# A macaron block on one Trainium2 core: feed-forward products by seven block products in place of eight

## The chip, the core and the metric

The kernel runs on one core of a Trainium2 chip. The time is device microseconds for one execution, the median of the runs shown. The engines are TensorE (PE), VectorE (DVE), ScalarE (ACT), GpSimd (POOL) and SyncE (SP, which issues DMAs). Each runs its own instructions in order; semaphores join them, and DMAs go through queues that SP, ACT or POOL feed.

## The reference

One sequence of 512 tokens with 1024 channels passes a feed-forward block, a mixer, a second feed-forward block and a last norm, all in float32:

```python
def swiglu(x, w_gate, w_up, w_down):
    return (jax.nn.silu(x @ w_gate) * (x @ w_up)) @ w_down
h = rms_norm(x, norm_ffn1[l])
x = x + 0.5 * swiglu(h, ffn1_gate[l], ffn1_up[l], ffn1_down[l])
...
x = x + mixed @ w_out[l]
h = rms_norm(x, norm_ffn2[l])
x = x + 0.5 * swiglu(h, ffn2_gate[l], ffn2_up[l], ffn2_down[l])
return rms_norm(x, norm_final)
```

The hidden width F is 2816, 22 tiles of 128. The mixer projects the normed rows with `w_in`, runs an RWKV-7 recurrence over 8 heads and a sliding-window attention side by side, and projects back with `w_out`; the change touches it only where its inputs come from.

## The kernel before

Each float32 factor of a product is split into a high part rounded to the matmul's format and a low part, the rest. A product is three matmuls into one PSUM bank (`mm3`, L452): high weights by high activations, high by low, low by high. Weights come in pieces of 512 KB (8 tiles of 128x128), loaded on SP's queue (`weights_load`, L402); ACT makes the high part (L409), DVE the low part (L410).

Channels lie on partitions, tokens along the free axis: a matmul holds a 128x128 weight tile and streams 128x512 activations. `ffn` (L467) goes over the hidden tiles in three parts (`PARTS`: 0 to 8, 8 to 16, 16 to 22). For each hidden tile it does the gate's and the up's eight k tiles, `gated` (L512) makes silu(gate) times up, split again; after a part, eight output tiles of down are accumulated and added to x (L508). The next norm's row sums ride along, and its scale is applied to gate and up. The last part of the second block is done in the layout of the output (`finish`, L530), with activations held and weights streamed, after transposing x (L541).

The order on PE, ACT and DVE is the program's (`MAN`); in the mixer PE's alone (`MAN1`). POOL's instructions are placed by the scheduler, so its 14 DMAs of small vectors (`vectors`, L153) go early though they stand late in the program. `want` and `take` keep two weight pieces ahead. In `start` (L207) the first tile's products (L252) are written in between the transposes of x (L233). `spill` (L595) and `unspill` keep x in memory across the mixer, as channels.

## Time and profile before

| | |
|---|---|
| runs | 1022.91, 1022.75, 1021.14 us; median 1022.75 |
| profiled execution | span 1023.7 us, which is its own time as far as the page tells it |
| first block | 0 to 376 us |
| mixer | 376 to 649 us |
| second block | 649 to 1023.7 us |

The page has the busy time of each engine over the span (part 1), its course in 40 slices with the granted PE clock in tenths, the share of the DMA engines and the rate (part 2), the queues (3), the chain of work that ended last (4), the costliest groups (5) and the DMA issues (6). A matmul's own time overlaps the next one's, so what one costs is the distance of two starts in the timeline. A wait is named by the instruction that waited and what released it.

### The profile page before, as it was taken

Reading aid. Unit: us, or ns where it says so; the run is one execution under the profiler, and the core shown is the slowest. Engines: PE = TensorE matmul, PEld = TensorE weight load, DVE = VectorE, ACT = ScalarE, POOL = GpSimd, SP = SyncE. Lnnn points to the kernel's source line nnn. Section 1 sums busy time; section 2 is a strip of 40 time slices with the busy share of each in tenths; the row PEclk is TensorE's granted clock in tenths of the full one; section 3 lists DMA queues with packets and bytes.
Section 4 is the critical chain, followed back from the end, with each engine's and each line's share of the span. In section 5 each row is a group of like instructions: output and inputs, shape, how many; then the busy total and the mean of one; then the engine's idle time right before and its main releaser. Section 6 shows DMA issues by size and latency. Waiting matters only on the chain. (4 is left out here: it accounts for less than half of the span.)

```text
span 1023.7 us, 12876 instructions
## 1 busy us (share of the span) xinstructions
PE 1008.6 (99%) x5123; PEld 824.8 (81%) x5123; DVE 557.8 (54%) x886; ACT 397.5 (39%) x631; POOL 52.2 (5%) x84
## 2 busy tenths in 40 slices
PE   8999999999999999999999999999999999999997
PEld 6888888888888887888867788788888888888886
DVE  5644424444344568799976686644443444424445
ACT  5422212332222447864376754432222322212343
POOL 6000000000000010120010120000000000000001
PEclk8999999999999999999989899999999999999999
DMA  8333333333233352313230323223333333333322
GB/s 207 103 101 87 100 103 92 94 103 101 85 102 93 103 176 62 94 51 78 77 84 22 93 63 103 81 87 101 102 97 88 103 101 88 101 103 90 96 83 83
DMA packets 174444, 96.82 MB, mean 95 GB/s; under 512 B 12334, under 2 KB 170096, under 8 KB 174384
## 3 DMA queue, kind: packets, MB, share of 16 engines
q1 hardware_dynamic: 172032, 90.19, 30.9%
q0 software_dynamic: 2336, 5.81, 2.0%
q8 instruction: 40, 0.66, 0.3%
q14 instruction: 20, 0.16, 0.1%
q10 hardware_dynamic: 16, 0.00, 0.0%
HBM read 89.43 MB, written 4.19 MB: 91 GB/s over the span
## 5 line engine op out<-in xcount | busy, mean ns | idle before, releaser
L457 PE MATMUL bpgu<-h_o,lo_bg 128*128 128x512 f32 x176 | 69.3, 394 | 0.0
L455 PE MATMUL bpgu<-h_o,hi_bg 128*128 128x512 f32 x176 | 69.2, 393 | 0.0
L456 PE MATMUL bpgu<-h_o,hi_bg 128*128 128x512 f32 x176 | 69.0, 392 | 0.0
L455 PE MATMUL apd<-h_a,hi_ad 128*128 128x512 f32 x176 | 68.6, 390 | 0.0
L456 PE MATMUL apd<-h_a,hi_ad 128*128 128x512 f32 x176 | 68.5, 389 | 0.0
L457 PE MATMUL apd<-h_a,lo_ad 128*128 128x512 f32 x176 | 68.5, 389 | 0.0
L457 PE MATMUL bpgu<-h_o,lo_bu 128*128 128x512 f32 x176 | 68.5, 389 | 0.0
L455 PE MATMUL bpgu<-h_o,hi_bu 128*128 128x512 f32 x176 | 68.5, 389 | 0.0
L456 PE MATMUL bpgu<-h_o,hi_bu 128*128 128x512 f32 x176 | 68.5, 389 | 0.0
L457 PE MATMUL apgu<-h_x,lo_au 128*128 128x512 f32 x168 | 65.5, 390 | 0.0
L455 PE MATMUL apgu<-h_x,hi_ag 128*128 128x512 f32 x168 | 65.5, 390 | 0.0
L455 PE MATMUL apgu<-h_x,hi_au 128*128 128x512 f32 x168 | 65.4, 390 | 0.0
L456 PE MATMUL apgu<-h_x,hi_au 128*128 128x512 f32 x168 | 65.4, 389 | 0.0
L457 PE MATMUL apgu<-h_x,lo_ag 128*128 128x512 f32 x168 | 65.4, 389 | 0.0
L456 PE MATMUL apgu<-h_x,hi_ag 128*128 128x512 f32 x168 | 65.4, 389 | 0.0
L409 ACT ACTIVATE hi_bu<-raw_bu 128x1024 fp32r<-128x1024 f32 x22 | 23.4, 1061 | 87.0 <-PE bpgu L456 78.3
L409 ACT ACTIVATE hi_au<-raw_au 128x1024 fp32r<-128x1024 f32 x21 | 22.3, 1062 | 83.0 <-PE apgu L456 70.1
L516 DVE TENSOR_TENSOR sgb<-bpgu,rstd 128x512 f32<-128x512 f32 x22 | 15.2, 692 | 70.6 <-PE bpgu L457 69.4
L516 DVE TENSOR_TENSOR sga<-apgu,rstd 128x512 f32<-128x512 f32 x22 | 15.2, 691 | 69.2 <-PE apgu L457 66.4
L409 ACT ACTIVATE hi_ad<-raw_ad 128x1024 fp32r<-128x1024 f32 (+1 forms) x24 | 23.8, 991 | 74.9 <-PE apd L456 51.9
L455 PE MATMUL bpd<-h_b,hi_bd 128*128 128x512 f32 x128 | 49.8, 389 | 0.0
L456 PE MATMUL bpd<-h_b,hi_bd 128*128 128x512 f32 x128 | 49.8, 389 | 0.0
(427 smaller groups left out, 2348.3 us busy)
## 6 DMA issues: line engine op xcount, KB each, us to landing
raw_bg<-in_ffn_gate_dram SPq DMA_DIRECT2D x22, 512.0 KB, 3.8
raw_bu<-in_ffn_up_dram SPq DMA_DIRECT2D x22, 512.0 KB, 3.8
raw_ag<-in_ffn_gate_dram SPq DMA_DIRECT2D x21, 512.0 KB, 3.9
raw_au<-in_ffn_up_dram SPq DMA_DIRECT2D x21, 512.0 KB, 3.8
raw_ad<-in_ffn_down_dram SPq DMA_DIRECT2D x16, 512.0 KB, 4.0
raw_bd<-in_ffn_down_dram SPq DMA_DIRECT2D x16, 512.0 KB, 4.0
raw_o<-in_w_out_dram SPq DMA_DIRECT2D x16, 256.0 KB, 3.3
raw_ad<-in_ffn_down_dram SPq DMA_DIRECT2D x8, 384.0 KB, 3.6
```

Of the source, the lines that this page charges most:

```text
L409: nc.scalar.activation(hi[:, :n], raw[:, :n], AF.Copy)
L455: nc.tensor.matmul(ps, hi[:, k], ah, start=first, stop=False)
L456: nc.tensor.matmul(ps, hi[:, k], al, start=False, stop=False)
L457: nc.tensor.matmul(ps, lo[:, k], ah, start=False, stop=last)
L516: nc.vector.tensor_tensor(sg, pg, self.rstd, ALU.mult)
```

## The change

Each feed-forward product is done as a product of 2x2 blocks by seven block products in place of eight, M1 to M7, in the order of `PRODUCTS`. The activations' blocks are two halves of the tokens by two halves of the contraction. For gate and up, the weights' block columns are up and gate, so one pass gives both; hidden columns go in chunks of 512 (the sixth has 256), and a chunk is 14 steps of 12 matmuls. Then down runs as a second phase over all chunks, product by product; its block columns are the two halves of the output. Activations are now held (128 tokens by 128 channels) and weights streamed, 512 columns at a time (`mm3w`).

The sums of weight blocks are not made by an engine: the block that stands in SBUF is the target of accumulating DMAs from memory on POOL's queue (`Stream.add`). W22 is added to W12 right after its load, for M7; W11 once M7's low part is made, for M6; W21 after M6's, for M4; and W12 to W11 after M1's, for M5. A step's piece is loaded nine steps ahead (`LOADS`; five or more in down), its high part made three ahead, its low part two. In down the loads, other than M3's, stand on POOL's queue too. Sums of activation blocks are made on POOL (`operand_sum`, `down_sums`).

Results come with tokens on partitions: hidden rows are transposed on PE (16 per chunk), the row sums of the norms come from ACT's squares along the free axis, x is kept and spilled by token and loaded again from memory in the down phase (`early`), and its rows are transposed for the mixer. POOL and SP now keep the program's order too. The small vectors are loaded in step 20 of the first block.

Three places in the instruction order, each with what it waits for. First POOL where the first block's down phase begins. `r12a83` is the tile for W12 of M7's first piece (step 83), `ds83` its operand sum, `r11a81` W11 of M1's fifth, `xN` the rows of x. Before, POOL's entries at the end of that block were these:

```order
L344 TENSOR_TENSOR ms_342<-ms_342,pack_123 128x4 [waits DVE_49,Activation_49,Pool_49]
L595 DMA x_spill_2609<-xT0_167 128x512 [waits DMASW3_49,DVE_49]
L595 DMA x_spill_2609<-xT1_183 128x512 [waits DMASW4_49,DVE_49]
L595 DMA x_spill_2609<-xT2_201 128x512 [waits DMASW5_49,DVE_49]
L595 DMA x_spill_2609<-xT3_217 128x512 [waits DMASW6_49,DVE_49]
```

and now:

```order
L698 TENSOR_TENSOR ds83_1847<-hTa0_474 128x512
L140 DMA r12a83_1872<-in_ffn1_down_dram 128x2x512
L131 DMA r12a83_1872<-in_ffn1_down_dram 128x2x512 [waits DMASW5_49,DMASW4_49]
L131 DMA r11a81_1811<-in_ffn1_down_dram 128x2x512 [waits DMASW0_49,DVE_49,Activation_49]
L698 TENSOR_TENSOR ds84_1878<-hTa1_755 128x512
L140 DMA r12a84_1895<-in_ffn1_down_dram 128x2x512 [waits DMASW7_49]
L131 DMA r12a84_1895<-in_ffn1_down_dram 128x2x512 [waits DMASW7_49]
L131 DMA r11a82_1842<-in_ffn1_down_dram 128x512 [waits DMASW1_49,DMASW2_49,DVE_49,Activation_49]
L605 DMA xN0_228<-in_x_dram 128x1024
L605 DMA xN1_229<-in_x_dram 128x1024 [waits DMASW3_49,PE_49]
```

A load (L140) is followed at once by its add (L131), which waits for a semaphore of POOL's DMA queue; the pattern comes six times, with two more rows of `xN` between.

Second PE at the small vectors (`vec_ps`, their transpose). `Ya1` is the bank of M2 in chunk 1, `Xa1` that of M6, which follows in step 20. Before:

```order
L457 MATMUL apgu_312<-h_x_240,lo_au_276 128x512
L157 MATMUL vec_ps<-pack,vec_rows 128x64 [waits DMASW4_49,DMASW5_49,DMASW3_49,DMASW6_49,DMASW2_49,DMASW7_49,DMASW1_49,DMASW0_49]
L455 MATMUL apgu_406<-h_x_139,hi_ag_308 128x512 [waits Activation_49]
```

and now:

```order
L637 MATMUL Ya1_1_602<-loa_163,AaM2h_233 128x512
L268 MATMUL vec_ps_634<-pack0_128,vec_rows_619 128x64 [waits DMASW4_49,DMASW3_49,DMASW5_49,DMASW2_49,DMASW6_49,DMASW1_49,DMASW7_49,DMASW0_49,DVE_49]
L635 MATMUL Xa1_0_507<-hia_161,AaM6h_273 128x512 [waits Activation_49]
```

and on POOL, where the 14 loads now stand between accumulates (`rawaa`) of chunk 1 and, behind them, of chunk 2:

```order
L131 DMA rawaa_112<-in_ffn1_up_dram 128x2x512 [waits DMASW6_49,DMASW4_49,DVE_49]
L131 DMA rawaa_112<-in_ffn1_up_dram 128x2x512 [waits DMASW7_49,DMASW5_49,DVE_49]
L264 DMA vec_rows_619<-in_norm_mix_dram 8x128 [waits PE_49]
L264 DMA vec_rows_619<-in_norm_ffn2_dram 8x128
L264 DMA vec_rows_619<-in_rwkv_shift_mix_dram 14x128 [waits DMASW2_49]
```

The transpose stands at much the same place on PE as before; its loads moved on POOL from ahead of the first block's work to behind the accumulates.

Third PE at the start, where `xta31` is the last of the eight groups of transposes of x and `Xa0_0` the first bank of M1. Before, the first three product matmuls stood ahead of the fourth group:

```order
L252 MATMUL apgu0_130<-h_x0_139,hi_ag0_104 128x512 [waits PE_49,Activation_49]
L252 MATMUL apgu0_130<-h_x0_139,hi_ag0_104 128x512 [waits DVE_49]
L252 MATMUL apgu0_130<-h_x1_149,hi_ag0_104 128x512 [waits Activation_49]
L233 MATMUL xt_ps3_169<-pack_123,xin2_109 128x128 [waits DMAHW7_49]
```

and now:

```order
L526 MATMUL xta21_202<-pack0_128,xin2_108 128x128 [waits DMAHW5_49]
L526 MATMUL xta21_202<-pack0_128,xin2_108 128x128 x3
L526 MATMUL xta31_208<-pack0_128,xin3_109 128x128 [waits DMAHW6_49,DVE_49]
L526 MATMUL xta31_208<-pack0_128,xin3_109 128x128 x3
L635 MATMUL Xa0_0_237<-hia_161,AaM1h_149 128x512 [waits DVE_49,Activation_49]
```

All transposes of x moved ahead of the first product. The diff, cut to its core:

```diff
-MAN = {PE, ACT, DVE}
-MAN1 = {PE}
-PARTS = [(0, 8), (8, 16), (16, 22)]
+MAN = {PE, ACT, DVE, POOL, SP}
+PRODUCTS = ("M1", "M7", "M2", "M6", "M5", "M3", "M4")
+LOADS, LOADS_D, HIGH, LOW, HI, LO = 9, 5, 3, 2, 5, 4
+SUMS_AHEAD = 5
+OPERANDS = {"M2": (0, 0), "M6": (1, 2), "M5": (4, 4), "M3": (5, 6), "M4": (8, 8)}
+MAN1 = {PE, POOL, SP}
...
+class Stream:
...
+        for c in range(6):
+            n = min(S, F - c * S)
+            nk = 1024 // n
+            for m in PRODUCTS:
+                for idx in range(4 // nk):
+                    add("gu", c, m, idx, nk, n, lambda i, j, c=c, n=n, nk=nk, idx=idx:
+                        rows((wu, wg)[j], i * S + idx * nk * P, nk, c * S, n))
+        self.first_down = len(self.pieces)
+        for m in PRODUCTS:
+            for c in range(6):
+                nk = 2 if c < 5 else 1
+                add("d", c, m, c, nk, S, lambda i, j, c=c, nk=nk: rows(wd, c * S + i * nk * P, nk, j * S, S))
...
+    def add(self, pc, b, i, j):
+        self.nc.gpsimd.dma_start(self.raw[pc.kind, pc.c, pc.idx, b], pc.block(i, j), accum_op=ALU.add)
+    def loads(self, upto, by=None):
+        while self.loaded < min(upto, len(self.pieces)):
+            pc = self.pieces[self.loaded]
+            self.loaded += 1
+            b = {"M1": "11", "M7": "12", "M2": "21", "M3": "22"}.get(pc.m)
+            if b:
+                eng = self.nc.gpsimd if pc.kind == "d" and pc.m != "M3" else by or self.nc.sync
+                eng.dma_start(self.tile(pc, b), pc.block(int(b[0]) - 1, int(b[1]) - 1))
+            if pc.m == "M7":
+                self.add(pc, "12", 1, 1)
+    def high(self, q):
+        while self.highs <= min(q, len(self.pieces) - 1):
+            self.loads(self.highs + 1)
+            pc = self.pieces[self.highs]
+            b = {"M1": "11", "M5": "11", "M2": "21", "M3": "22"}.get(pc.m, "12")
+            raw = self.raw[pc.kind, pc.c, pc.idx, b]
+            hi = self.ring("hi", HI, F32R).next(pc.n)[:, :pc.nk]
+            self.nc.scalar.activation(hi, raw, AF.Copy)
+            self.his[pc.q] = raw, hi
+            self.highs += 1
+    def low(self, q):
+        while self.lows <= min(q, len(self.pieces) - 1):
+            pc = self.pieces[self.lows]
+            raw, hi = self.his[pc.q]
+            lo = self.ring("lo", LO, F32R).next(pc.n)[:, :pc.nk]
+            self.nc.vector.tensor_tensor(lo, raw, hi.bitcast(F32), ALU.subtract)
+            self.parts[pc.q] = hi, lo
+            if pc.m in ("M7", "M6", "M1"):
+                self.add(pc, *{"M7": ("12", 0, 0), "M6": ("12", 1, 0), "M1": ("11", 0, 1)}[pc.m])
+            self.lows += 1
...
+        a = self.a = self.stream("a")
+        load(0, 0)
+        load(1, 0)
+        a.loads(2)
+        load(2, 0)
+        load(3, 0)
+        a.loads(4)
+        load(0, 1)
+        load(1, 1)
+        a.loads(6)
+        load(2, 1)
+        load(3, 1)
+        self.consts()
+        self.first_gain()
+        self.ss = self.small("ss_a", 4, "ss")
+        self.operands_begin("a")
+        gain = self.gain1
+        for h in range(2):
+            for t in range(4):
+                self.operand_turn(xin[t], t, h, gain)
+                if h == 0 and t < 2:
+                    self.operand_split("M1", t)
+                if h == 0 and t == 1:
+                    a.split(0)
+                    a.split(1)
+            if h == 0:
+                self.operand_sum("M7")
+                self.operand_split("M7")
+                a.split(2)
+        for t in range(4):
+            self.row_squares(xin[t], t)
+        self.row_scales()
...
+    def ffn(self, tag):
+        st = self.b if tag == "b" else self.a
+        self.due = []
+        self.banks = {}
+        self.hT = {}
+        self.temps = {}
+        self.gtr = Ring(self.f, "gt" + tag, 8, F32, S)
+        if tag == "a":
+            self.xN = self.new_rows()
+        n = len(st.pieces)
+        for q in range(n):
+            pc = st.pieces[q]
+            st.loads(min(q + LOADS, max(q + LOADS_D, st.first_down, 2 * q - st.first_down)))
+            st.high(q + HIGH)
+            st.low(q + LOW)
+            self.early(tag, st, q)
+            if pc.kind == "gu":
+                self.gu_step(st, pc)
+            else:
+                self.down_step(st, pc)
+            while self.due and self.due[0][0] <= q:
+                self.due.pop(0)[1]()
+    def early(self, tag, st, q):
+        for m, (a, b) in OPERANDS.items():
+            if q == a:
+                self.operand_sum(m)
+            if q == b:
+                self.operand_split(m)
+        if tag == "a" and q == 20:
+            self.vectors()
+        if tag == "a" and q == len(st.pieces) - 8:
+            self.consts_mix()
+        if q == st.first_down + 3:
+            if tag == "b":
+                self.xN = self.new_rows()
+            for t in range(4):
+                self.nc.gpsimd.dma_start(self.xN[t], self.I["x"][0, t * P:(t + 1) * P] if tag == "a" else self.xd2[t])
+        for k in range(st.first_down, len(st.pieces)):
+            if q == max(k - SUMS_AHEAD, st.first_down - 2):
+                self.down_sums(st.pieces[k])
+        k = q + LOW
+        if st.first_down <= k < len(st.pieces) or q == st.first_down - 1:
+            for k in range(st.first_down, k + 1) if q == st.first_down - 1 else (k,):
+                self.down_split(st.pieces[k])
+    def gu_step(self, st, pc):
+        nc = self.nc
+        m, c, tag = pc.m, pc.c, st.tag
+        hi, lo = self.A[m]
+        pieces = [p for p in st.group(pc)]
+        both = len(pieces) == 1
+        for i in (0, 1) if both else (pc.idx,):
+            b = self.bank(f"{tag}{c}", m, i)[:, :pc.n]
+            ts = slice(i * P, i * P + P)
+            first, last = m in ("M1", "M7", "M2"), m in ("M3", "M4", "M2")
+            k = 0
+            for p in pieces:
+                bh, bl = st.parts[p.q]
+                for kk in range(p.nk):
+                    self.mm3w(b, hi[:, k, ts], lo[:, k, ts], bh[:, kk], bl[:, kk], first and k == 0, last and k == 3)
...
+    def mm3w(self, ps, ah, al, bh, bl, first, last):
+        mm = self.nc.tensor.matmul
+        mm(ps, ah, bh, start=first, stop=False, skip_group_check=True)
+        mm(ps, al, bh, start=False, stop=False, skip_group_check=True)
+        mm(ps, ah, bl, start=False, stop=last, skip_group_check=True)
+    def down_sums(self, pc):
+        if pc.m not in ("M7", "M6", "M3"):
+            return
+        eng = self.nc.gpsimd
+        (a11, a12), (a21, a22) = self.down_blocks(pc.c)
+        if pc.m == "M7":
+            self.ds[pc.c] = self.f.tile([P, 2, 256], F32, tag="ds", name=f"ds{pc.q}", bufs=5)[:, :pc.nk]
+            eng.tensor_tensor(self.ds[pc.c], a11, a21, ALU.subtract)
+        elif pc.m == "M6":
+            eng.tensor_tensor(a21, a22, a21, ALU.subtract)
+            eng.tensor_tensor(a11, a11, a21, ALU.add)
+        elif pc.m == "M3":
+            eng.tensor_tensor(a12, a11, a12, ALU.subtract)
+    def down_step(self, st, pc):
+        m, c, tag = pc.m, pc.c, st.tag
+        first, last = m in ("M1", "M7", "M2"), m in ("M3", "M4", "M2")
+        if c == 0:
+            for i in range(2):
+                self.bank(f"{tag}d", m, i) if first else None
+        if c == 4:
+            return
+        todo = [(p, i) for i in range(2) for p in ((st.pieces[pc.q - 1], pc) if c == 5 else (pc,))]
+        for p, i in todo:
+            b = self.bank_of(m, i)
+            hi, lo = self.D[p.q]
+            bh, bl = st.parts[p.q]
+            ts = slice(i * P, i * P + P)
+            for kk in range(p.nk):
+                self.mm3w(b, hi[:, kk, ts], lo[:, kk, ts], bh[:, kk], bl[:, kk], first and p.c == 0 and kk == 0, last and p.c == 5)
+        if c == 5:
+            for i in range(2):
+                self.down_post(m, i)
+        if m == "M4":
+            (self.tail_a if tag == "a" else self.tail_b)(c)
...
+    def between(self, gain):
+        self.first_pts = []
+        ws = []
+        def part(i, ks):
+            for k in ks:
+                self.mm3(self.first_pts[i], ws[i], k, self.xh[k], k == 4, k == 3)
+        for i in range(2):
+            ws.append(self.take("in_" + RWKV_TILES[i][0]))
+            self.first_pts.append(self.psum("in_ps_" + RWKV_TILES[i][0]))
+            part(i, range(4, 8))
+        for j in range(4):
+            self.turn_rows(j, gain)
+        for t in (2, 3):
+            self.row_squares(self.xN[t], t)
+        self.row_scales()
+        part(0, range(4))
+        self.want()
+        self.stats_spread()
+        part(1, range(4))
```

## Rows read from the trace of the kernel before

**Rows 1.** The page's part 1, whole span: busy time, share and instructions of each engine.

```profile
PE 1008.6 (99%) x5123; PEld 824.8 (81%) x5123; DVE 557.8 (54%) x886; ACT 397.5 (39%) x631; POOL 52.2 (5%) x84
```

**Rows 2.** PE's waits, whole span: tile, line, releaser; total us, times, longest.

```profile
PE xt_ps L233 <- DMA xin<-in_x_dram: 3.4, 2, 2.3
...
PE pu L1036 <- ACT pack L1030: 0.2, 1, 0.2
```

**Rows 3.** PE's timeline late in block two: start, us, engine, line, operation, shapes, count.

```profile
954.89 0.39 PE L456 MATMUL bpgu<-h_o,hi_bu 128*128 128x512 f32 x1
...
957.16 0.39 PE L457 MATMUL bpgu<-h_o,lo_bu 128*128 128x512 f32 x1
...
980.51 3.65 PE L541 MATMUL xn_ps<-pack,xr 128*128 128x128 f32 x32
984.06 0.50 PE L548 MATMUL e<-hi_be,h_b 128*128 128x512 f32 x1
...
1012.79 0.28 PE L548 MATMUL e<-hi_be,h_b 128*128 128x256 f32 x1
...
1013.15 0.28 PE L548 MATMUL e<-hi_be,h_b 128*128 128x256 f32 x1
```

**Rows 4.** The page's part 2: DMA share in tenths and GB/s, 40 slices.

```profile
DMA  8333333333233352313230323223333333333322
GB/s 207 103 101 87 100 103 92 94 103 101 85 102 93 103 176 62 94 51 78 77 84 22 93 63 103 81 87 101 102 97 88 103 101 88 101 103 90 96 83 83
```

**Rows 5.** Busy by window: us, busy of each engine, PEclk, DMA share, GB/s.

```profile
6.00:12.00 6.00, 3.28 (x14) 2.62 (x15) 2.92 (x5) 2.67 (x5) 5.81 (x11) 0.70 1.19 280
12.00:20.00 8.00, 8.00 (x37) 6.56 (x37) 6.26 (x11) 5.73 (x11) 4.84 (x13) 0.80 1.16 267
26.00:90.00 64.00, 64.00 (x289) 52.78 (x288) 33.34 (x47) 22.78 (x30) 1.87 (x1) 1.00 0.34 99
566.00:570.00 4.00, 4.00 (x28) 2.71 (x27) 1.13 (x5) 3.35 (x12) 0.79 (x2) 0.77 0.92 326
```

**Rows 6.** Groups by line and form, ACT and DVE: busy us, mean ns, idle before.

```profile
L409 ACT ACTIVATE hi_bg<-raw_bg 128x1024 fp32r<-128x1024 f32 x22 | 23.3, 1061 | 51.2 <-PE bpgu L456 31.6 <-PE bpd L456 8.8 <-issue 7.1
...
L410 DVE TENSOR_TENSOR lo_bg<-raw_bg,hi_bg 128x1024 fp32r<-128x1024 f32 x22 | 27.0, 1225 | 41.3 <-ACT hi_bg L409 41.3
```

**Rows 7.** PE's timeline at the start: the first product, and the second tile's first.

```profile
10.14 1.63 PE L252 MATMUL apgu<-h_x,hi_ag 128*128 128x512 f32 x3
...
25.81 0.39 PE L455 MATMUL apgu<-h_x,hi_ag 128*128 128x512 f32 x1
```

**Rows 8.** POOL's timeline at the start, and one spill issue at the first block's end.

```profile
4.24 0.53 POOL L191 MEMSET pack<- 128x512 f32 x1
...
8.46 0.56 POOL L153 DMA_DIRECT2D vec_rows<-in_norm_mix_dram  x1
...
17.48 1.98 POOL L153 DMA_DIRECT2D vec_rows<-in_b_in_attn_dram  x4 [0.94 <-DMA lraw<-in_rwkv_a_dram]
...
352.81 0.54 POOL L595 DMA_DIRECT2D x_spill<-xT  x1 [2.55 <-DVE xT L508]
```

**Rows 9.** DMA issues: queue, count, KB each, median us from issue to landing.

```profile
raw_bg<-in_ffn_gate_dram SPq DMA_DIRECT2D x22, 512.0 KB, 3.8
...
xin<-in_x_dram SPq DMA_DIRECT2D x8, 256.0 KB, 5.8
x_spill<-xT POOLq DMA_DIRECT2D x8, 256.0 KB, 2.5
...
nf<-in_norm_final_dram POOLq DMA_DIRECT2D x1, 512.0 KB, 5.0
...
lraw<-in_rwkv_a_dram POOLq DMA_DIRECT2D x2, 128.0 KB, 6.2
g<-in_rwkv_g_dram POOLq DMA_DIRECT2D x1, 256.0 KB, 3.6
...
vec_rows<-in_b_in_attn_dram POOLq DMA_DIRECT2D x2, 0.5 KB, 3.8
```

More of the change, by code (lines that the diff above doesn't have):

```diff
@@ L155, in vectors @@
             r += k
[L156 removed]
+        pt = self.tp("vec_ps", (P, S))
         nc.tensor.transpose(pt[:, :n], raw, self.ident[:n, :n])
@@ L1273, in out_mix @@
+        x = self.xN[t][:, h * S:h * S + S]
+        self.nc.vector.tensor_tensor(x, self.wo[m], x, ALU.add)
     def out_mix(self, next_gain):
-        self.xh = []
-        for m in range(ND):
-            if m % 2 == 0:
-                w = self.take(f"o1_{m // 2}")
+        st = self.b = self.stream("b")
+        self.operands_begin("b")
+        self.ss = self.small("ss_b", 4, "ss")
+        self.xd2 = self.dram.tile([4, P, D], F32, name="x2_spill")
+        c = self.col[next_gain]
+        gain = self.vec[:, c:c + 8]
@@ new lines, in turn @@
+        def turn(m):
+            t, h = m % 4, m // 4
+            self.operand_turn(self.xN[t], t, h, gain)
+            if h == 0:
+                if t < 2:
+                    self.operand_split("M1", t)
+                if t == 3:
+                    self.operand_sum("M7", self.nc.vector)
+                    self.operand_split("M7")
+            else:
+                self.row_squares(self.xN[t], t)
+                self.nc.gpsimd.dma_start(self.xd2[t], self.xN[t])
+        w = {}
+        for m in range(8):
+            t, h = m % 4, m // 4
+            if t == 0:
+                for kp in range(2):
+                    w[kp] = self.take(f"o1_{2 * h + kp}")
+            ps = self.wo[m] = self.acc(f"wo1_{m}")
+            for k in range(4):
+                self.out_product(ps, self.mixed, w[k // 2], t, k, k == 0, k == 3)
+            if m in (0, 1) and self.plan:
@@ L1288, in block @@
         n.make_plan()
-        n.start(I["x"])
-        n.ffn("a", "norm_mix")
-        n.mixer("norm_ffn2")
-        n.ffn("b", None, I["ffn2_down"])
+        man = lambda: tc.manual_schedule(engines=MAN_F)
+        with tc.manual_schedule(engines=MAN1):
+            with man():
+                n.start(I["x"])
+                n.ffn("a")
+                n.between("norm_mix")
+            n.mixer()
+            with man():
+                n.out_mix("norm_ffn2")
+                n.ffn("b")
+                n.finish()
 _INS = ["x", "norm_ffn1", "ffn1_gate", "ffn1_up", "ffn1_down", "norm_mix", "w_in", "b_in_attn", "rwkv_shift_mix",
```

574 lines of the change are left out of this document (286 added, 288 removed).

## The prediction

> **What bounds the kernel now.** I read the page's busy times first. TensorE (PE) is busy for 99% of the span, its weight loads overlap it, and GpSimd (POOL) has 52 us of work in the whole run [rows 1]. The list of PE's waits comes second: the largest of its six entries is 3.4 us, on the loads of x at the start, the smallest 0.2, and all six make under 9 us [rows 2]. So time before is PE's products at their pitch, and whatever the change does to the time, it does either by the number of products or by making PE wait. The pitch comes from the timeline: eleven 128x512 matmuls start between 954.89 and 957.16, 0.227 us apart; 256-wide ones follow at 0.12, and 32 transposes of 128x128 fill the 3.55 us from 980.51 to 984.06, 0.111 each [rows 3]. Data is far from a limit: about 100 GB/s and a third of the DMA engines' time in the steady feed-forward stretch [rows 4], against 326 GB/s at a share of 0.92 in the busiest short stretch of the run [rows 5].
>
> I sum against the profiled execution (span 1023.7 us), which lies 0.95 us above the median of the three runs.
>
> **PE's work, -68 us.** Before, the feed-forward blocks issue 3150 matmuls of 512 columns and 36 of 256: 3150 x 0.227 + 36 x 0.12, with the unrounded 0.2267, is 718.4 us. After, each block has five chunks of 168, a last chunk of 168 at 256 columns, and 462 for down: 2604 and 336 in both, 630.6 us. That is -87.8. New transposes turn the products' results: 88 for each block's hidden rows and 32 for the rows that the mixer takes, 208; against them the 32 small matmuls of the old row sums and their spread leave. The net 176 x 0.111 is +19.5 [rows 3]. The later x transposes replace those of the old output part one for one. PE: **-68.3**.
>
> **Splitting the weights, nothing.** Each block now splits 119 pieces in place of 66, at 1.06 us on ScalarE (ACT) and 1.23 on VectorE (DVE) [rows 6]. In a chunk of 14 steps, 38.1 us of products and 1.8 of transposes, that is 15 and 17 us, and with evacuations of half that size neither passes 25 of 39.9. PE's products cover it, and HIGH and LOW put it three and two steps (8 and 5 us) ahead. If a weight arrives late, this cover is gone and 2.3 us lie on the path.
>
> **Start, +9.** Before, the first tile's 48 products (10.9 us) begin at 10.14, between arriving halves of x, and are done at 25.81: 14.9 us lost [rows 7]. After, all eight groups of transposes stand ahead of the first product on PE, and the last two loads of x are queued on SP behind six weight pieces. Until then 2.1 MB of x, 3.1 MB of weights and 1.05 MB of accumulates move; at 280 GB/s [rows 5] this is 22.4 us after an issue at about 1.6, so the first product comes at 24 in place of the 14.9: +9. Without the accumulates it is +5; with them read twice at 267 GB/s, +14.
>
> **Small vectors, +12.** Fourteen DMAs of vector rows were issued on POOL from 8.46 to 19.46 us, 0.51 each and 11.0 with POOL's own waits, and hidden: PE's transpose of them came later and waited for nothing [rows 2, 8]. Now they are issued in step 20 of the first block, in program order behind accumulates that wait for VectorE, and PE's transpose vec_ps stands between the products of step 19 and 20. So PE waits for all: 11.0 + 3.8 landing [rows 9] less one step of head start, 2.7: **+12.1**. Behind it the next accumulates are late, which the steps ahead still cover. Lower end: 7.1 of pure issue with two steps of start, 5.5.
>
> **Down phase, +29 for each block.** Here POOL is in order. For each of M7's six pieces it forms an operand sum, issues the load of W12, waits until that load has landed, and only then issues the add of W22 and whatever comes next. Between PE's arrival at down and M7's last piece stand 21 DMA issues at 0.55 (11.6, from the 0.54 of a spill issue [rows 8]), five and a half operand sums, six landings, the last add's landing, and its split (2.3). For the sums the trace has no row; a memset of the same tile takes 0.53 [rows 8], a sum reads two tiles, so I take 1.06 and 5.8 in all. With L for a landing this chain is 19.7 + 7L. PE has M1's products (15.0) and M7's first four pieces (10.9) to do meanwhile, 25.9, so it waits 7L - 6.2 in each block. Nothing on ACT, SP or DVE is late instead: M2's loads come next in POOL's queue and are due one chain later.
>
> L is bounded by rows of POOL's queue: 2.5 for a spill (256 KB, to memory), 3.6 for g (256 KB into SBUF), 5.0 for nf (512 KB into SBUF), 6.2 for lraw in the busy first microseconds [rows 9]. A weight piece is 512 KB into SBUF, as nf, so I take 5.0: 28.8 each, **+57.6**; the ends are 11.3 and 37.2 each. The Trainium skill, page "DMA: Bandwidth & Descriptors", section "Anatomy of one DMA - SWDGE (gpsimd) path", fits about 2.0 us plus bytes/436e3, 3.2 us for such a piece; by it the waits would be 16.2 each and the sum 25 us lower, 1031. The trace's nf, at 5.0, does not agree with that, so it stays outside my sum.
>
> **Traffic in gate/up, +10.** A chunk now moves 4.2 MB of loads and 4.2 MB of accumulates in 39.9 us, 211 GB/s in place of 99 [rows 5]. If an add costs what a load costs, this is 60% of the 354 GB/s that 326 at 0.92 stands for, and nothing waits but an occasional late piece: lower end 0. If an add costs two loads, the same chunk is worth 12.6 MB: 36 us at 354 GB/s, but 45 us at the 280 of the start [rows 5], which is 5.1 us for each of eleven full chunks, +56. I take **+10**, nearer to the first: adds have three steps (8.2 us) from their issue until ScalarE reads the sum, and the loads of the busy start land in 5.8 [rows 9].
>
> **Between blocks, +6; clock, +7.** After the last down product the mixer's rows are turned, scaled twice and squared: eight 128x512 copies at half of 1.06, two squares at 1.06, two evacuations at half of 1.23, 7.5 us, of which the first projections' 24 products (5.4) can hide some: 2 to 7.5, taken 6. After PE's idle time at the start the granted clock was 0.70 over 6 us and 0.80 over the next 8 [rows 5], means between the full 2.4 GHz and the 1.2 below it, and 1.8 and 1.6 us of full speed lost. Four long waits (vectors, two downs, the mixer) at 1.7 are +7; ends 2 and 20.
>
> **Sum:** -68.3 + 9 + 12 + 57.6 + 10 + 6 + 7 = +33, that is 1057 against the span of 1023.7, and **1056** against the median.
>
> **Rivals.** *The POOL chain is short (faster).* With all else as taken the change breaks even at 2 x (7L - 6.2) = 24, L = 2.6; with adds that cost nothing extra and no clock lost (-15) at L = 3.7. For it: g lands in 3.6 and the weights' own loads on SP in 3.8 [rows 9]. Against it: POOL's only 512 KB load took 5.0 in a quieter stretch than this. With L = 2.5 and neither extra it gives 1007. Chance 0.25. *Adds pace the gate/up stretch.* A sum in place must read what it adds to, so its bytes may count twice: +56 in place of +10, and adds that land in 7.5 cost down another 5: 1108. The Trainium skill, page "Collectives: The Full Stack", part 3, on why ReduceScatter is half of AllGather, says that an add takes two source reads on one ring and so runs at half the rate; that speaks against this change, and by it this rival holds. No row before shows an add at all. For it otherwise: the share is already 1.19 in the start at 280 GB/s [rows 5]. Against: a 36 us chunk would still fit under 39.9. Chance 0.17. *No change to be measured*: the waits just eat the 68 us saved, 0.03. That the change does not do what it says I exclude: the counts above are those of the built program. My forecast keeps 0.55.
>
> **Range.** About 0.2% is what a measurement can tell here. Faster takes the first rival, 0.25; same 0.03; slower the rest, 0.72. Low ends with L = 3.6 (start +5, vectors +5.5, down +38, nothing for traffic, +2, +2) give 1008; high ends (traffic +56, L = 6.2) 1120. From 1003 to 1130 leaves out some 0.1 on either side.
>
> **What would show it.** Right: PE busy near 940 us, waits listed on M7's products in both down phases near 29 us each, released by VectorE's lo and behind it by a POOL DMA; a gap of some 12 us at vec_ps; POOL's timeline with a load, an idle stretch of L, an add, six times over. Wrong: down phases with gaps under 12 us each (L overrated); gate/up steps that wait all along at a DMA share near 1 (the second rival); or PE's pitch itself changed.

## The result and the profile after

The changed kernel takes 1171.49 us (median of four runs, 1169.9 to 1176.27) against 1022.39 for the kernel before on the same chip: a ratio of 1.148 [1.145, 1.1511]. The direction was predicted, the size was not: 1056 had been forecast, at most 1130. The profiled execution has a span of 1174.6 us. Against the span before and the 68.3 us of products saved, 1174.6 - 1023.7 + 68.3 = 219 us of loss has to be found where the prediction had 102.

The page of the changed kernel, parts 1 and 2:

```profile
span 1174.6 us, 13568 instructions
PE 1004.7 (86%) x5053; PEld 805.1 (69%) x5053; DVE 711.2 (61%) x990; ACT 569.8 (49%) x891; POOL 325.0 (28%) x314
PE   5796999998357798699999999989999998446897
PEclk9797999999668898799998999989999999767989
DMA  9597798937777621512211153978988947868601
```

Three things differ from [rows 1]. PE is idle for 170 us where it was idle for 15. It is also busy for 1004.7 us where the count of products gave 940, so its instructions took 65 us longer; the clock's digits are low just where PE's are. And POOL has six times its old work. PE's list of waits, its longest entries (us in total, times, longest):

```profile
PE Qad L635 <- ACT dd L561: 32.4, 6, 8.3
PE Qbd L635 <- ACT dd L561: 29.7, 5, 9.4
PE Xbd L635 <- ACT dd L561: 12.4, 2, 11.4
PE gain_ps L237 <- POOL pack L224: 10.8, 1, 10.8
PE Xad L635 <- ACT dd L561: 10.6, 2, 9.7
PE vec_ps L268 <- DMA vec_rows<-in_b_in_attn_dram: 10.3, 1, 10.3
PE Xad L635 <- DVE xN L743: 6.9, 1, 6.9
PE Xbd L635 <- DVE xN L743: 6.7, 1, 6.7
...
PE Yb L637 <- DVE lob L160: 4.1, 1, 4.1
```

In [rows 2] the longest was 3.4. `Qad` and `Qbd` are M7's banks in the two down phases, which M4 uses again (2.2 of the 32.4 us lie there; M7 has five long waits in either block); `Xad` and `Xbd` are first M1's (released by ACT's split of an activation block, `dd`), later M6's (released by `xN`). By stretch (length, then PE, PEld, DVE, ACT and POOL busy, granted clock, DMA share, GB/s):

```profile
21.00:76.00 55.00, 45.78 (x184) 35.38 (x182) 36.81 (x39) 33.06 (x42) 22.04 (x15) 0.88 0.80 187
76.00:129.00 53.00, 42.68 (x184) 34.63 (x182) 23.46 (x25) 21.97 (x28) 16.31 (x23) 0.87 0.75 164
130.00:170.00 40.00, 40.00 (x186) 33.09 (x185) 23.39 (x25) 21.95 (x29) 9.62 (x9) 1.00 0.92 210
275.00:312.00 37.00, 20.49 (x80) 14.88 (x78) 11.62 (x16) 8.42 (x15) 16.95 (x18) 0.85 0.83 176
312.00:368.00 56.00, 29.26 (x67) 20.11 (x68) 17.51 (x16) 11.48 (x16) 29.40 (x28) 0.65 0.83 213
383.00:438.00 55.00, 47.36 (x200) 38.12 (x199) 46.89 (x46) 26.07 (x37) 24.86 (x33) 0.94 0.43 84
1025.00:1080.00 55.00, 28.89 (x68) 19.91 (x69) 17.44 (x16) 11.17 (x16) 30.21 (x28) 0.63 0.79 192
```

These are chunk 0, chunk 1, a steady chunk, M1 of down, M7 of down, M6 with M5 and M3, and M7 of the second block. A steady chunk takes 40.0 us with PE busy throughout, as the prediction's 39.9 has it. So the saving is there; the other rows are where more than three times as much is lost. From the first matmul of each stage in the timeline, against a product at full pitch (15.0 us for 66 matmuls):

| stretch | at full pitch | took | loss | the prediction's term |
|---|---|---|---|---|
| start and chunk 0 | 14.9 + 40.0 | 21.5 + 54.5 | 21.1 | +9 |
| chunk 1, with the small vectors | 40.0 | 53.4 | 13.4 | +12 |
| other gate/up, both blocks | | | 13.6 | +10 |
| M1 of down | 2 x 15.0 | 37.0 + 38.4 | 45.4 | 0 |
| M7 of down | 2 x 15.0 | 55.3 + 54.5 | 79.8 | +57.6 |
| M6, M5, M3 of down | 2 x 45 | 54.9 + 54.6 | 19.5 | 0 |
| M2, M4 of down | 2 x 30 + 1.4 | 39.1 + 31.2 | 8.9 | 0 |
| mixer | 273.1 | 292.9 | 19.8 | +6 |
| clock (in the rows above) | | | | +7 |

The sum is 221 against the 219 of the spans. Down alone is 154.

POOL's queue in M7 of the first block, from its timeline (start, duration, idle time before and what ended it):

```profile
313.43 0.75 POOL L140 DMA_DIRECT2D r12a<-in_ffn_down_dram  x1 [3.03 <-DVE dd L562]
318.75 2.51 POOL L131 DMA_DIRECT2D r12a<-in_ffn_down_dram  x2 [4.57 <-DMA r12a<-in_ffn_down_dram]
320.28 2.28 POOL L698 TENSOR_TENSOR ds<-hTa 128x512 f32<-128x512 f32 x1
321.49 1.76 POOL L140 DMA_DIRECT2D r12a<-in_ffn_down_dram  x1
329.24 2.43 POOL L131 DMA_DIRECT2D r12a<-in_ffn_down_dram  x2 [6.00 <-DMA r12a<-in_ffn_down_dram]
...
339.73 1.19 POOL L131 DMA_DIRECT2D r12a<-in_ffn_down_dram  x1 [6.08 <-DMA r12a<-in_ffn_down_dram]
```

It is the predicted pattern: operand sum (L698), load (L140), about 6 us of idle time until it lands, add (L131). A round takes 10.5 us, for 2.5 us of products. By the prediction's prices (3.5 issues of 0.55, a sum of 0.97 on the average, L of 5.0) it would be 7.9. The load at 313.43 came 3.0 us later still, behind VectorE. And on PE, what a wait does to the products behind it: the fourth of the six pieces from 347.23, half of the fifth behind it, the last from 361.30.

```profile
347.23 0.80 PE L635 MATMUL Qad<-hia,dd 128*128 128x512 f32 x1 [5.04 <-ACT dd L561]
...
349.41 0.63 PE L636 MATMUL Qad<-hia,dd 128*128 128x512 f32 x1
349.83 0.63 PE L637 MATMUL Qad<-loa,dd 128*128 128x512 f32 x1
...
353.42 0.39 PE L635 MATMUL Qad<-hia,dd 128*128 128x512 f32 x1
353.65 0.40 PE L636 MATMUL Qad<-hia,dd 128*128 128x512 f32 x1
...
361.30 0.79 PE L635 MATMUL Qad<-hia,dd 128*128 128x512 f32 x1 [7.02 <-ACT dd L561]
```

The pitch behind the wait is 0.43, nearly twice that of [rows 3], at a granted clock of 0.50 (348 to 351 us). It comes back to 0.23 from 351.89 on, with eight products left until the next wait; behind the three waits before this one it stays at 0.43 up to the last of the twelve products or the one before.

What these waits name is ACT's split of an activation block (`dd`), not a weight. ACT's order has the split for a piece behind the high part of the next piece's weights (`high` runs three steps ahead, the splits two), and that high part waits until its load or add has landed. ACT's rows in the first block, and one of PE's:

```profile
288.34 0.63 ACT L151 ACTIVATE hia<-r11a 128x512 fp32r<-128x512 f32 x1 [1.02 <-DMA r11a<-in_ffn_down_dram]
300.69 1.06 ACT L151 ACTIVATE hia<-r12a 128x1024 fp32r<-128x1024 f32 x1 [11.20 <-DMA r12a<-in_ffn_down_dram]
301.65 0.40 ACT L561 ACTIVATE dd<-hTa 128x256 fp32r<-128x256 f32 x1
302.11 0.79 PE L635 MATMUL Xad<-hia,dd 128*128 128x512 f32 x1 [9.68 <-ACT dd L561]
...
350.92 0.63 ACT L151 ACTIVATE hia<-r12a 128x512 fp32r<-128x512 f32 x1 [3.74 <-DMA r12a<-in_ffn_down_dram]
359.89 1.06 ACT L151 ACTIVATE hia<-r21a 128x1024 fp32r<-128x1024 f32 x1 [7.82 <-DMA r21a<-in_ffn_down_dram]
360.85 0.40 ACT L561 ACTIVATE dd<-ds 128x256 fp32r<-128x256 f32 x1
```

M1's last weights had their high part at 288.34, but its last products waited until 302.11, when M7's first add had landed. M7's last weights had theirs at 350.92, but the products waited until 361.30, when M2's first piece had landed. The second block has the same two waits, of 11.4 and 4.0 us.

### The profile page after: what moved, and what is told of

The parts are those of the page before. It is cut to its first block, busy times and chain, and to the rows that moved or that the text cites. A ratio compares the mean times of both kernels' runs of the same rounds, so it can differ in the third digit from the quotient of the medians.

```text
span 1174.6 us, 13568 instructions
## 1 busy us (share of the span) xinstructions
PE 1004.7 (86%) x5053; PEld 805.1 (69%) x5053; DVE 711.2 (61%) x990; ACT 569.8 (49%) x891; POOL 325.0 (28%) x314
## 5 line engine op out<-in xcount | busy, mean ns | idle before, releaser
L160 DVE TENSOR_TENSOR loa<-rawaa,hia 128x1024 fp32r<-128x1024 f32 x55 | 68.2, 1253 | 13.6 <-ACT hia L151 9.6
L160 DVE TENSOR_TENSOR lob<-rawab,hib 128x1024 fp32r<-128x1024 f32 x55 | 67.3, 1236 | 13.1 <-ACT hib L151 7.8
L151 ACT ACTIVATE hia<-rawaa 128x1024 fp32r<-128x1024 f32 x55 | 57.3, 1051 | 31.9 <-DMA rawaa<-in_ffn_up_dram 16.9
L151 ACT ACTIVATE hib<-rawab 128x1024 fp32r<-128x1024 f32 x55 | 57.4, 1051 | 30.8 <-DMA rawab<-in_ffn_up_dram 14.9
L562 DVE TENSOR_TENSOR dd<-ds,dd 128x512 fp32r<-128x512 f32 (+1 forms) x12 | 10.5, 874 | 93.2 <-ACT dd L561 93.2
L131 POOL DMA_DIRECT2D rawab<-in_ffn_gate_dram x22 | 27.2, 1248 | 115.8 <-DVE lob L160 47.8
L131 POOL DMA_DIRECT2D rawaa<-in_ffn_gate_dram x22 | 27.5, 1255 | 110.3 <-DVE loa L160 54.0
L635 PE MATMUL Xbd<-hib,dd 128*128 128x512 f32 x88 | 37.0, 421 | 19.2 <-ACT dd L561 12.4
L635 PE MATMUL Qad<-hia,dd 128*128 128x512 f32 x44 | 24.0, 546 | 32.4 <-ACT dd L561 32.4
L635 PE MATMUL Xad<-hia,dd 128*128 128x512 f32 x88 | 36.5, 415 | 17.4 <-ACT dd L561 10.6
L131 POOL DMA_DIRECT2D rawaa<-in_ffn_up_dram x22 | 26.8, 1230 | 74.7 <-DVE loa L160 54.6
L131 POOL DMA_DIRECT2D rawab<-in_ffn_up_dram x22 | 26.8, 1250 | 69.9 <-DVE lob L160 58.8
L562 DVE TENSOR_TENSOR dd<-hTb,dd 128x512 fp32r<-128x512 f32 (+1 forms) x31 | 29.1, 942 | 22.1 <-ACT dd L561 22.1
L562 DVE TENSOR_TENSOR dd<-hTa,dd 128x512 fp32r<-128x512 f32 (+1 forms) x31 | 29.8, 963 | 19.9 <-ACT dd L561 19.9
L160 DVE TENSOR_TENSOR lob<-rawbb,hib 128x1024 fp32r<-128x1024 f32 x22 | 26.9, 1222 | 19.3 <-ACT hib L151 19.3
L636 PE MATMUL Xad<-hia,dd 128*128 128x512 f32 x88 | 36.3, 412 | 1.9 <-DVE dd L562 1.1
L635 PEld LDWEIGHTS Qad<-hia,dd 128*128 128x128 f32 x44 | 11.4, 260 | 37.8 <-ACT dd L561 35.3
```

Source lines behind the costliest of these rows:

```text
L131: self.nc.gpsimd.dma_start(self.raw[pc.kind, pc.c, pc.idx, b], pc.block(i, j), accum_op=ALU.add)
L151: self.nc.scalar.activation(hi, raw, AF.Copy)
L160: self.nc.vector.tensor_tensor(lo, raw, hi.bitcast(F32), ALU.subtract)
L562: nc.vector.tensor_tensor(lo, src, hi.bitcast(F32), ALU.subtract)
L635: mm(ps, ah, bh, start=first, stop=False, skip_group_check=True)
L636: mm(ps, al, bh, start=False, stop=False, skip_group_check=True)
```

## The experiments

The first theory was that down is bound by POOL's order: loads, adds and sums in one queue, each add behind a landing. The rival was that the adds' bytes bind the DMA engines, in whatever order they are issued. Runs 1 to 8 are one execution each, so a difference of a few microseconds between them says little; the kernel before took 1021.23 beside 1, 2, 3 and 5, and 1019.18 beside 4, 6, 7 and 8.

**1. M7's and M2's loads from SP.** Nothing else moves; POOL still waits for each landing, but the next loads are under way meanwhile.

```diff
-eng = self.nc.gpsimd if pc.kind == "d" and pc.m != "M3" else by or self.nc.sync
+eng = {"M1": self.nc.gpsimd, "M7": self.nc.sync, "M2": self.nc.sync, "M3": self.nc.sync}[pc.m] if pc.kind == "d" else by or self.nc.sync
```

> In the down phases the loads of W12 (M7) and W21 (M2) go on SP's queue, M1's stay on POOL's; all accumulates stay where they are. Theory 1 (POOL's order: load, wait for its landing, add, six times over): the add finds its load landed, M7 falls from 55 us towards 25 in each block, the whole from 1171 to about 1110. Theory 2 (traffic: accumulates keep the DMA engines at a share of 0.8 in M1 and M7 whatever the order): M7 stays above 45 us, the whole above 1150, with the share of the DMA engines unchanged or higher.

Measured 1113.32: 58 us less. M7 fell from 55.3 and 54.5 to 25.8 and 28.1. M1 and M7 of the first block by window, and M7's waits, in this run:

```profile
274.00:308.00 34.00, 24.18 (x77) 16.94 (x77) 13.27 (x17) 9.06 (x16) 19.63 (x20) 0.75 1.09 290
308.00:334.00 26.00, 19.05 (x67) 13.99 (x67) 13.99 (x16) 10.66 (x15) 13.52 (x12) 0.87 1.03 201
PE Qad L635 <- ACT dd L561: 8.7, 3, 5.3
```

The waits on M7's bank fell from 32.4 to 8.7 us with the same bytes moved (2.2 of either in M4). So the order of the loads did cost most of M7's loss. M1 gained only 3.1 and 4.6 us, and the DMA share is now over 1: the next limit is already in sight.

**2. M1's loads off POOL as well**, from ACT's queue (`"M1": self.nc.scalar`).

> As the run before, and M1's loads in down are issued on ACT's queue, so that none of the down phase's loads stands in POOL's order. Theory 1: M1 falls too, from 37 us towards 20 in each block, the whole to about 1080. Theory 2: the bytes are the same, so M1 and M7 together stay above 80 us of the 92 in each block.

Measured 1120.04, no gain over the first run. M1 went from 33.9 to 31.1 and 33.8 to 30.5, not to 15; gate/up became longer (253.2 to 257.0, 230.4 to 235.9), perhaps by ACT's issues, which no run tried apart. M1 with all its loads free of POOL still takes twice its products, and the trace shows why. Its largest wait, 7.9 us in the first block, is the one of ACT's order: M1's last high part was made at 290.25, then ACT waited 9.2 us for M7's first piece, and the split of M1's last block came behind it.

**3. The adds of down cut to 16 of 512 columns**, order kept: nearly the whole sum of weight blocks is left out in down, and so are its bytes.

```diff
+        if pc.kind == "d":
+            raw, src = raw[:, :, 0:16], src[:, :, 0:16]
```

> The accumulates of the down phases add 16 of 512 columns only: the sums of the weight blocks are left out except there, the order, the number of DMAs and all waits stay. Theory 1: POOL still waits for each load, only the landing is shorter (from 6.5 towards 4 us without an add ahead of it in the queue), so M7 falls from 55 to about 40 us and the whole to about 1135. Theory 2: without the bytes M7 and M1 come near their 15 us of products, 20 to 25 each, the whole to about 1060.

Measured 1130.83. M1 26.8 and 26.2, M7 39.8 and 44.5: without the adds' bytes the order still costs 25 to 30 us in each M7, and with them another 10 to 15.

**4. Both**, tiny adds and loads from SP.

> Both parts of the two runs before at once: M7's and M2's loads on SP's queue, and the down phase's adds cut to 16 of 512 columns (the sums of weight blocks in down are left out but for these). With the loads off POOL's order alone, M1 and M7 took 34 and 26 us at a share of the DMA engines above 1. Theory 1 and 2 together (the order is one cause, the bytes of the adds what is left): M1 and M7 now fall to 20 and 17 us, the whole to about 1067. Rival, what is left in M1 and M7 is neither but the clock and the splits on ACT and DVE: they stay within 3 us of 34 and 26.

Measured 1086.09; M1 22.1 and 23.1, M7 24.0 and 23.7. From 37 and 55 us, order and bytes together explain all but 7 to 9 us over the products; the whole is 19 us above the forecast. What remains has no large wait (the longest on M7 is 3.1).

**5. The start.** The constants stand first on POOL, and the small vectors are loaded by SP at the end of `start`; only their transpose stays in step 20.

```diff
+        self.consts()
         a = self.a = self.stream("a")
...
-        self.consts()
...
+        self.vectors()
...
         if tag == "a" and q == 20:
-            self.vectors()
+            self.vectors_turn()
```

> The constants (the identity above all) are made before the first weight loads, so that on POOL they stand ahead of the first adds, and the 14 loads of small vectors go on SP's queue at the end of the start; their transpose on PE stays in step 20. If POOL's order is what costs here: the first transposes of x move from 15.5 to about 8 us, the first product from 21.5 to about 17, and the wait of 10.3 us at vec_ps is gone, in all 12 to 17 us off. If the start is bound by the bytes that must land, the first chunk still ends at 76 us and only the 10 us at vec_ps go.

Measured 1149.58, 22 us less. The transposes of x begin at 4.7 us in place of 15.5, yet the first product comes at 21.7 as before, since PE now waits 9.4 us for x itself. The 22 us come from the first block's gate/up (254.0 to 231.6): chunk 1 is free of its wait of 10.3 us, and M7 of chunk 0 waits no more for weights (6.3 us before). M2 still does, 3.9 us. In the changed kernel POOL's first adds stood ahead of the identity that the transposes need:

```profile
11.99 2.61 POOL L131 DMA_DIRECT2D rawaa<-in_ffn_gate_dram  x2 [11.49 <-DMA rawaa<-in_ffn_gate_dram]
14.90 0.29 POOL L224 TENSOR_SCALAR_AFFINE_SELECT pack<-pack 128x128 f32<-128x128 f32 x1
```

**6. Plain loads for the adds of gate/up**: the sums of weight blocks are left out there, with as many bytes read.

```diff
-        self.nc.gpsimd.dma_start(self.raw[pc.kind, pc.c, pc.idx, b], pc.block(i, j), accum_op=ALU.add)
+        self.nc.gpsimd.dma_start(self.raw[pc.kind, pc.c, pc.idx, b], pc.block(i, j), **({"accum_op": ALU.add} if pc.kind == "d" else {}))
```

> In gate and up every accumulating DMA is a plain load of the same block into the same tile (the weight sums are left out there), with the same bytes, order and waits. It prices the add: in the steady chunks the DMA engines were at a share of 0.92 and PE never waited. If an add costs the engines two loads, the share falls to about 0.62 and PE's 40.0 us for a chunk stay; if an add costs one load, the share stays near 0.9. The first chunk (54.5 us) falls towards 45 us if the price of adds is what it waits for.

Measured 1159.35. The same steady chunk as above, in this run:

```profile
130.00:170.00 40.00, 40.00 (x187) 33.11 (x185) 23.38 (x25) 21.96 (x29) 5.76 (x9) 1.00 0.64 210
```

The share falls from 0.92 to 0.64 at the same 210 GB/s, and PE does not notice. Sixteen plain transfers fill 0.64 x 40 = 25.6 us of all engines, 1.6 each; eight loads and eight adds 36.8, so an add costs 3.0: 1.9 loads. The gain lies elsewhere: 5.0 us in the last chunk, where loads for down already compete, 5.7 in the second block's gate/up, 1.7 and 2.2 in the first two chunks. The first chunk stays at 52.8, so it is not the price of adds that it waits for.

**7. The activation sums of down on VectorE**, with runs 1 and 5 (`eng = self.nc.vector` in `down_sums`).

> M7's and M2's loads in down on SP's queue, the start's order as in the run before, and the sums of the hidden blocks in down on VectorE in place of POOL. On POOL's side M6, M5 and M3 took 54.5 us for 45 of products, with VectorE's splits at 2 us beside POOL's sums and 0.7 without, and one of 7.5. If POOL's sums slow VectorE, these three fall to 46 to 48 us and their wait for the sum in x (7.4) goes, the whole is 1113 - 22 - 14 = about 1077. If VectorE is just full there (46 of 55 us busy), 22 sums of 0.7 add to it: 56 us or more, the whole above 1090.

Measured 1078.13. M6, M5 and M3 fell from 54.9 and 54.6 to 45.4 and 45.3, their full pitch, although VectorE now does more. Run 1, with POOL's sums, has 54.4 and 55.1 there. The cause shows in VectorE's rows. In the changed kernel, beside POOL's sums (VectorE's rows, then POOL's):

```profile
384.07 3.46 DVE L160 TENSOR_TENSOR loa<-r12a,hia 128x1024 fp32r<-128x1024 f32 x1
389.15 2.53 DVE L160 TENSOR_TENSOR loa<-r12a,hia 128x1024 fp32r<-128x1024 f32 x1
395.42 1.21 DVE L160 TENSOR_TENSOR loa<-r11a,hia 128x1024 fp32r<-128x1024 f32 x1
396.55 7.52 DVE L562 TENSOR_TENSOR dd<-hTa,dd 128x512 fp32r<-128x512 f32 x1
...
384.70 1.73 POOL L700 TENSOR_TENSOR hTa<-hTa 128x512 f32<-128x512 f32 x1
386.51 2.16 POOL L701 TENSOR_TENSOR hTa<-hTa 128x512 f32<-128x512 f32 x1
...
396.30 7.22 POOL L703 TENSOR_TENSOR hTa<-hTa 128x512 f32<-128x512 f32 x6
```

and in run 7, with the sums (L706 is one) on VectorE itself:

```profile
321.69 0.68 DVE L706 TENSOR_TENSOR hTa<-hTa 128x512 f32<-128x512 f32 x1
323.01 0.69 DVE L568 TENSOR_TENSOR dd<-hTa,dd 128x512 fp32r<-128x512 f32 x1
...
325.88 1.22 DVE L160 TENSOR_TENSOR loa<-r12a,hia 128x1024 fp32r<-128x1024 f32 x1
```

A split of 0.69 us took 7.52 while six sums ran on POOL; it ended half a microsecond after the sixth.

**8. Down by eight products**: gate/up as in the change with run 5's start, down with plain loads, held activations and 528 matmuls of 512 columns. No adds and no sums are left in down.

```diff
-        for m in PRODUCTS:
-            for c in range(6):
-                nk = 2 if c < 5 else 1
-                add("d", c, m, c, nk, S, lambda i, j, c=c, nk=nk: rows(wd, c * S + i * nk * P, nk, j * S, S))
+        for h in (1, 0):
+            for kp in range(11):
+                add("d", kp // 2, "D", (h, kp), 2, S, lambda i, j, h=h, kp=kp: rows(wd, kp * 2 * P, 2, h * S, S))
```

> One part of the change undone: gate and up stay by seven products, down is done by plain products (528 matmuls in a block in place of 462) over two output halves, still with activations held, without sums of any kind and with plain loads of 512 KB per 5.4 us of products on POOL's queue; the start's order as in the run before. If the sums and the adds of down are the cause, a down phase takes 122 to 126 us in place of 186 and 179, the whole about 1025 to 1035. If the phase itself (hidden rows turned, split again, loads near the transition) is what costs, a down phase stays above 140.

Measured 1028.52. Down takes 124.2 and 123.6 us in place of 186 and 179: the eighth product is 15 us dearer at pitch and 55 to 62 us cheaper in fact. Against run 7, the best down by seven here that keeps all its sums (145 and 142 us), it is 21 and 18 us cheaper. This is 9 us above the kernel before, with a first chunk still 7.2 us over its pitch.

**9. The short chunk second, hidden rows split once, the mixer's rows turned between projections.** In this and the next run down reads, for the short chunk, hidden rows that another chunk had since replaced; the work is the same.

> As down_by_eight, with three small moves at its seams: the 256-wide chunk comes second in gate and up (the last chunk before down is a full one, whose evacuations have 38 us of products beside them), the first pieces of the hidden rows are split once and not twice at the start of down, and the last four turned rows for the mixer come between products of two projections, not ahead of all. The seams lost 3.6 and 1.9 us in each block and 8 us at the mixer's entry. If latency behind short work is the cause, 8 to 12 us go: 1017 to 1021, level with the kernel before or just under it. If they only move to where the short chunk now stands, at most 4 us go.

Measured 1033.33, a ratio of 1.0124 [1.0098, 1.0149]: a miss. The stall of the short chunk went with it to its new place (waits of 6.6 us on ACT's `gtb` in the second block), and the mixer's entry, from its first projection to the first of `in_ps_r`, got no shorter (28.9 us against 27.4).

**10. As 9, with the second half of x turned after M1.**

> As down_by_eight_2, and the second half of x is turned between M1's and M7's products in place of ahead of all (with its squares later): PE's first product no longer waits for the last loads of x. The first product comes at about 14 us in place of 21.5. If the first chunk is bound by what must land (2.1 MB of x and its weights and adds, the DMA engines at a share near 1 in the first 30 us), the second chunk starts within 2 us of where it did and the whole is 0 to 2 us less; if PE's order cost the wait, 5 to 7 us less, about 1012.

Measured 1032.7, 1.0108 [1.0091, 1.0125]. The first product comes at 10.5 in place of 21.7, and the second chunk starts at 69.5 against 69.1. That is the time of the first alternative. But the trace does not show its cause alone: PE's longest wait in the chunk, 5.8 us at 46.60 in M6, is on a low part whose high part (42.95) stood on ACT behind the four row squares that this run moved there (37.85 to 42.00). So whether the start is bound by what must land stays open.

**11. The short chunk last again; M6's operands split later; the mixer's rows by high parts first.**

```diff
-OPERANDS = {"M2": (0, 0), "M6": (1, 2), "M5": (4, 4), "M3": (5, 6), "M4": (8, 8)}
+OPERANDS = {"M2": (0, 0), "M6": (1, 4), "M5": (5, 5), "M3": (6, 7), "M4": (8, 8)}
...
+            st.high(q + (2 if (p.kind, p.c) == ("gu", 5) else HIGH))
```

> As down_by_eight (short chunk last again), with four moves: M6's operands are split two steps later, so that VectorE no longer waits for POOL's sums ahead of M2's weight split (the waits of 4.4 and 4.1 us of PE on lo in M2, once in each block, should go); in the short chunk the high parts are made two steps ahead and not three, so that an add that is late does not stand ahead of an evacuation on ACT; the hidden rows' first pieces are split once; at the mixer's entry ACT makes the four rows' high parts first and copies x after. From 1028.5: 8 us for the first, 2 to 4 for the second and third, 3 to 4 for the last: 1012 to 1017, faster than the kernel before by 0.5 to 0.9%. If VectorE is simply full in the first chunk, the waits only move and the whole stays at 1023 or above.

Measured 1019.68, 0.9986 [0.9968, 1.0003]: above the 1012 to 1017 expected, and level with the kernel before as far as this interval tells. M2's waits for its low parts (4.4 and 4.1) are gone. The weights made later in the short chunk were a mistake: its waits grew to 5.4 and 3.6, and the mixer's third weight came 3.8 late.

**12. As 11, with the short chunk's weights three steps ahead again and the third mixer piece from POOL's queue** (`if kp == 5: self.weng = self.nc.gpsimd`).

> As down_by_eight_4, but in the short chunk the high parts are made three steps ahead again (with two its wait for the evacuation of x's bank had grown from 1.2 to 5.4 and 3.6 us), and the third weight piece of the mixer is loaded from POOL's queue, where it is issued as soon as the row scales are made, in place of ACT's, where it stood behind four copies and PE waited 4.3 us for it. If these two waits are what was given back there, 8 to 10 us go, with what the clock loses behind each: 1008 to 1013, faster than the kernel before by 0.9 to 1.3%. If the short chunk's adds are late whatever the order, only the 4 us at the mixer go: 1015.

Measured 1017.02 (12 runs, 1009.47 to 1021.34) against 1021.91, a ratio of 0.9951 [0.993, 0.9973]. This beats both kernels, the one before by 0.5%, less than expected. From the profiled execution, one of 1013.25 us, the busy times and the largest entry of PE's waits:

```profile
PE 976.5 (97%) x5185; PEld 799.9 (79%) x5185; DVE 641.8 (63%) x897; ACT 535.4 (53%) x817; POOL 207.2 (20%) x213
PE xta L530 <- DMA xin<-in_x_dram: 9.0, 4, 2.9
```

## Why the prediction was right, and where it failed

- **PE's work, -68**: right. A steady chunk has 40.0 us against 39.9 and no wait; splitting weights cost nothing there.
- **Start, +9**: too small. The first product at 21.5 was even sooner than the 24 taken. The step that failed is that the delay ended there: chunk 0 lost 14.5 more, waiting for weights in M7 and M2. `start` issues the first adds on POOL ahead of `consts` and so of the identity matrix, and I did not price that. Run 5 shows both: with POOL's order mended the first product stays at 21.7, where PE waits for x to land, and the chunk's loss falls from 14.5 to 6.9. Of these, M2's wait of some 4 us goes in run 11, with VectorE's order.
- **Small vectors, +12**: right in mechanism and size, 10.3 us of wait and 13.4 with the clock. With the loads moved ahead (run 5) the wait is gone.
- **Down, +57.6**: POOL's chain was rightly seen, and run 1 shows that it costs most of M7, but M7 measured 79.8 and the down phases 154. That is 96 of the 117 us that the forecast lacked. M7's idle time, 31.0 and 30.9 us, looks like the forecast 28.8 and is so by offsetting errors. From PE's arrival at down (275.49) to M7's last piece (361.30) the chain took 86 us where 19.7 + 7 x 5.0 = 54.7 was reckoned. POOL sat idle 4.6 to 6.3 us in that block between a load and its add, its issues cost 0.75 and not 0.55, its sums 2.2 and not 1.06, a round 10.5. PE's cover grew as well, because M1, taken as 15 us of free work, took 37 and 38. By run 3 the adds' bytes are worth 10 to 15 us of each M7 and 10 to 12 of each M1.
- **"Nothing on ACT, SP or DVE is late instead"**: the step of the down phase that failed outright. *ACT*: the prediction has M2's loads due one chain later, but M2's first piece stands on ACT ahead of M7's last split, and M7's first ahead of M1's last. These two waits make 9.7 of M1's 11.5 us of idle time and 7.0 of M7's 31.0, and 11.4 of 12.9 and 4.0 of 30.9 in the second block. So the waits named ACT's `dd` where the prediction expected VectorE's low part. No run changes ACT's order, so what it alone costs stays open: with it mended, part of M1's wait may come back in M7. *DVE*: M6, M5 and M3 lost 19.5 us, because POOL's activation sums held VectorE's splits up (run 7).
- **Traffic in gate/up, +10**: 13.6 measured, but not as an occasional late piece in steady chunks, which wait for nothing at a share of 0.92. With plain loads (run 6) the last chunks lose 5.0 and 3.6 us less and the entry of the second block 2.1. The wait of 4.1 us at that entry is not traffic: 3.1 of it stay in run 6, and it goes in run 11, where VectorE no longer waits for POOL's sums ahead of M2's weights.
- **Clock, +7**: the term most wrongly sized. PE is busy for 65 us beyond the count. I priced four long waits at 1.7 each. Each M7 has five waits of 4.0 to 9.4 us, each followed by products at half the pitch; the granted clock is 0.65 and 0.63 over the whole 55 us. So beside the waits stand slow products: M7 lost 79.8, of which 61.9 was idle, M1 45.4 with 24.4 idle, 39 us for the two together.
- **Between blocks, +6**: 19.8 measured. The entry, from the first projection to the first of `in_ps_r`, took 36.8 us in place of 19.3. Run 8 has 27.4, with down by eight and the squares and scales earlier; run 12 has 23.2, with other copies first and an earlier weight too. No run tried these alone, so what each of the turns, scales and late weights costs stays open.
- **Rivals**: POOL's chain was not short: the first rival stood on L near 2.5, and POOL waited 4.6 to 6.3 us in the first block, 4.1 to 8.4 in the second. (Its 1007 still holds 2 us of clock; with none lost it would be 1005 against the span.) The adds do cost two loads, as the second rival had it, but they did not pace gate/up. The Trainium skill, page "Collectives: The Full Stack", part 3, states for ReduceScatter that an add takes two source reads and so runs at half the rate; the 1.9 loads of run 6 agree with that. By the fit of the Trainium skill, page "DMA: Bandwidth & Descriptors" (section "Anatomy of one DMA — SWDGE (gpsimd) path"), a piece is estimated at 3.2 us. The 4.1 to 8.4 us between a load and its add here do not agree with that, nor do the 4.1 us (median) from issue to landing in run 8's first down phase, where no add runs.

## What to carry to other kernels

When a wait is put on an in-order queue, price the whole queue, and then every other in-order engine that waits for what it brings. Whatever stands behind such a wait is late as well: here the small splits on ACT that stood behind the next piece's weights, also those of the stage that was to cover the wait. A stall that is cut into many pieces between short runs of products costs PE's clock besides, here 39 us beside 86 us of idle time in M1 and M7. And the one block product in eight that this saves is worth taking only where its sums are free: in the steady chunks of gate/up they were. In down, with 2.5 us of products for each piece, plain loads and the eighth product were 55 to 62 us a block cheaper than the change as made, and 18 to 21 cheaper than run 7. A down by seven with ACT's splits ahead of the weights was not tried.

## What the runs showed of the hardware

- An accumulating DMA of 512 KB takes the DMA engines 3.0 us where a plain one takes 1.6 (run 6 against the changed kernel, same bytes and time).
- POOL's two-input sums hold up VectorE's two-input splits: 0.69 us became 7.52, 1.21 became 3.46 and 2.53 (run 7 takes it away). The Trainium skill, page "SBUF — State Buffer", section "Who interferes with whom", says that a VectorE instruction with two SBUF inputs contends with a GpSimd one that reads SBUF, and that the lock on the shared ports is exclusive. The trace agrees that they contend; the split of 7.52 us here stood through six sums, not one.
- In the two M7, after each of the waits of 4.0 to 9.4 us, PE ran at a pitch of 0.43 for most of the 12 to 18 products that followed, against 0.227 in [rows 3]. The granted clock was 0.50 from 348 to 351 us, the 1.2 GHz level, and 1.00, the 2.4 GHz level, from 352 to 354.
